# One change to a decoder-layer kernel on Trainium2: the down projection as a block product in seven products, with stored operand sums

## Chip, cores and metric

The kernel runs on one core of one Trainium2 chip. The metric is the device time of one execution in microseconds, the median of several runs.

## What is computed

One decoder layer for one sequence of 1024 tokens, width 1024, in fp32. Ahead of the part that matters here stand two attention groups, an output projection and a first layer norm. The change lies in the feed-forward block at the end, cut here to its core (D_FF = 2816):

```python
x  = layer_norm(ALPHA * x + (1 + gate_m) * y, ln1_g, ln1_b)
u2 = x * (1.0 + scale_f) + shift_f
h  = silu(u2 @ w_gate) * (u2 @ w_up)          # 1024 x 2816
y2 = h @ w_down                               # 1024 x 1024, inner dimension 2816
x  = layer_norm(ALPHA * x + (1 + gate_f) * y2, ln2_g, ln2_b)
```

## The kernel before

**Precision.** An fp32 matrix product is made from operands that are split in two: `split` (lines 86 to 88) has ScalarE cast a tile to the matmul type (`hi`, line 87) and VectorE subtract that from the tile (`lo`, line 88, two inputs in SBUF). Each product of two 128-row tiles then takes three matmuls (hi·hi, hi·lo, lo·hi), each 128x128 by 128x512.

**Gate/up.** The 2816 features are done in 22 groups of 128. Gate and up projection together are already a block product in seven products (`group_parts`, lines 1003 to 1051): 84 matmuls a group at line 996. For the next group `sum_weights` (lines 977 to 989) makes sums of weight blocks on VectorE (lines 982 to 985) and splits them. The results are put together in the tile `hf` by VectorE (lines 1032, 1040, 1042, 1043, 1047, 1048), and line 1049 stores `hf`, the hidden activations of 128 features by 1024 tokens, to DRAM (`h_d`).

**Down projection.** `ffn_down(half)` is called twice, for 512 tokens each. The eight PSUM accumulators are four row blocks q of 128 tokens by two column halves d of 512. A loop over 11 pairs of feature groups loads a pair of h back from `h_d` (line 1088) and both column halves of the matching 256 rows of w_down, splits these three tiles of 128x1024, and issues 48 matmuls (lines 1096 to 1098):

```python
h = (slot(HHI[n], (2, 512), dt=F32R, name="hh"), slot(HLO[n], (2, 512), dt=F32R, name="hl"))
load_h(i, *h)
w = [load_split((2, 512), w_src(i, d)) for d in range(2)]
for q in range(4):
    for d in range(2):
        mms(i, q, d, h, w[d])
```

That makes 2 x 11 x 48 = 1056 matmuls, and w_down is loaded twice. The last three pairs of a pass are kept in SBUF and multiplied one row block after the other, so that each row block ends by itself; then VectorE takes it out of PSUM times `gf` = 1 + gate_f (line 1138), adds it to ALPHA times the residual row (line 1139), takes statistics (line 824), and `out_norm` makes the layer norm and stores it (VectorE lines 829, 830, 1148, 1155; GpSimd's power for the inverse root, line 831, and its add at line 1153; ScalarE line 1152).

**The residual rows.** `rows_in(half)` (lines 1063 to 1072) loads four row blocks of z_d, the first layer norm without its gain and bias, and GpSimd multiplies by `l1g` (line 1069) and adds `l1b` (line 1070). Over both halves these are 16 GpSimd instructions of 128x1024.

**What sets the order.** The code is written in loops, but a scheduler arranges the instructions of each engine ahead of time; each engine then works in its fixed order and waits at semaphores. All loads and stores are issued in order from one queue (SP). Where a tile's place in SBUF (a numbered slot, or a pool's buffer) is used again, the load into it waits for the last reader.

Of the kernel before, what the change touches and what calls it, by code (L numbers as in the profile page):

```python
# [33 lines left out]
def hymba_layer_kernel(  # L34
# [967 lines left out]

    def group_parts(f, w):

# [17 lines left out]

        def p754():
            if f == 2:
                st_["h"] = slot(6 + par, (2, 512), name="hf")
# [31 lines left out]
    ROWS = ((0, 1, 2, 3), (10, 11, 12, 13))
    HRAW, HHI, HLO = (34, 35), (8, 16, 18), (9, 17, 19)
    NKEEP = 3
    KEPT = ((26, 27, 28, 29, 30, 31), (20, 21, 22, 23, 36, 37), (32, 33, 24, 25, 4, 5))  # L1060
# [13 lines left out]
    def ffn_down(half, between=()):
        last = half == 1
        between = list(between)
        wides = [wide(f"w{i}", "dn") for i in range(2)]
        acc = []
        for q in range(4):
            for d in range(2):  # L1080
                if q < 2:
                    acc.append(wides[q][:, d * 512 : (d + 1) * 512])
                else:
                    acc.append(bank(f"b{2 * (q - 2) + d}", "dn"))

        def load_h(i, hi, lo):
            raw = slot(HRAW[pc[0] % 2], (2, 512), name="hr")
            nc.sync.dma_start(raw, h_d[i][:, :, half * 512 : (half + 1) * 512].rearrange("f p n -> p f n"))
            split(hi, lo, raw)

        def mms(i, q, d, h, w):
            qs = slice(q * P, (q + 1) * P)
            for a in range(2):
                hh, hl, wh, wl = h[0][:, a, qs], h[1][:, a, qs], w[0][:, a, :], w[1][:, a, :]
                ps = acc[2 * q + d]
                nc.tensor.matmul(ps, hh, wh, start=i == 0 and a == 0, stop=False)  # L1096
                nc.tensor.matmul(ps, hh, wl, start=False, stop=False)  # L1097
                nc.tensor.matmul(ps, hl, wh, start=False, stop=i == NF // 2 - 1 and a == 1)  # L1098

        def w_src(i, d):  # L1100
            return w_down[i * 256 : (i + 1) * 256, d * 512 : (d + 1) * 512].rearrange("(k p) n -> p k n", p=P)

        for i in range(NF // 2 - NKEEP):
            n = pc[0] % 3
            h = (slot(HHI[n], (2, 512), dt=F32R, name="hh"), slot(HLO[n], (2, 512), dt=F32R, name="hl"))
            load_h(i, *h)
            pc[0] += 1
            w = [load_split((2, 512), w_src(i, d)) for d in range(2)]
            for q in range(4):
                for d in range(2):  # L1110
                    mms(i, q, d, h, w[d])
            if between:
                between.pop(0)()
        kept = []
        for n in range(NKEEP):
            i = NF // 2 - NKEEP + n
            ks = KEPT[n]
            h = (slot(ks[0], (2, 512), dt=F32R, name="kh"), slot(ks[1], (2, 512), dt=F32R, name="kl"))
            load_h(i, *h)
            pc[0] += 1  # L1120
            w = []
            for d in range(2):
                raw = wtile("raw", (2, 512), F32)
                nc.sync.dma_start(raw, w_src(i, d))
                hi = slot(ks[2 + 2 * d], (2, 512), dt=F32R, name="kwh")
                lo = slot(ks[3 + 2 * d], (2, 512), dt=F32R, name="kwl")
                split(hi, lo, raw)
                w.append((hi, lo))
            kept.append((i, h, w))
        rt = rows[half]  # L1130
        for q in range(4):
            bs = new_bs()
            for d in range(2):
                hs = slice(d * 512, (d + 1) * 512)
                for i, h, w in kept:
                    mms(i, q, d, h, w[d])
                tmp = tmp512("tmp")
                nc.vector.tensor_tensor(tmp, acc[2 * q + d], gf[:, hs], op=ALU.mult)
                nc.vector.scalar_tensor_tensor(
                    rt[q][:, hs], rt[q][:, hs], ALPHA, tmp, op0=ALU.mult, op1=ALU.add  # L1140
                )
                ln_stats(rt[q], d, bs)
            out_norm(half, q, rt[q], bs)
# [127 lines left out]
```

## Time and profile before

| | |
|---|---|
| Median of 3 runs | 1306.38 us (1302.6 to 1308.12) |
| Profiled execution | 1304.18 us, of which span 1302.4 us |
| Busy in the span | TensorE 96%, VectorE 58%, ScalarE 38%, GpSimd 20% |
| Mean granted TensorE clock | 0.996 of full speed |
| Gate/up, first matmul | 606.6 us |
| Down projection, first and last matmul | 1043.8 us, 1293.3 us |

Times in the trace count from the start of the span. PE is TensorE's matmul, DVE is VectorE, ACT is ScalarE, POOL is GpSimd, SP the queue that issues the loads and stores. A matmul's own duration (0.39 us) is longer than the distance between two starts, since they are pipelined; what a matmul costs is that distance.

### The profile page before, as it was taken

How to read it: one execution, taken by the hardware profiler on the slowest of the kernel's cores; microseconds unless marked ns; L12 is line 12 of the kernel's file. 1: busy time of each engine (PE TensorE's matmuls, PEld its weight loads, DVE VectorE, ACT ScalarE, POOL GpSimd, SP SyncE). 2: the span in 40 equal slices, each digit the busy share in tenths (PEclk: the TensorE clock that was granted, in tenths of full speed). 3: DMA queues.
4: the chain of work that ended last, by engine and by line, in shares of the span. 5: the costliest groups of instructions: out<-in, count | busy, mean ns of one | idle time of the engine just before them, and what ended most of it. 6: DMA issues, size and time to landing. Idle time of an engine off the chain costs nothing.

```text
span 1302.4 us, 16377 instructions
## 1 busy us (share of the span) xinstructions
PE 1256.3 (96%) x6341; PEld 1017.0 (78%) x6341; DVE 756.9 (58%) x1101; ACT 489.2 (38%) x826; POOL 259.6 (20%) x252
## 2 busy tenths in 40 slices
PE   5999999999999999998899999999999999999997
PEld 4888987899877656667688888888888888788885
DVE  7656537732465465456966565565566587483346
ACT  3422355523354465565633233233233333411331
POOL 3500023320255255331000000000000087010004
PEclk9999999999999999999999999999999999999999
DMA  9865621112125214144242331331231475643431
GB/s 299 260 226 180 213 65 34 27 23 66 50 91 145 74 34 147 65 145 130 82 144 81 98 96 51 96 97 54 93 97 49 167 267 164 201 153 116 148 111 65
DMA packets 124686, 153.17 MB, mean 118 GB/s; under 512 B 6608, under 2 KB 86586, under 8 KB 124608
## 3 DMA queue, kind: packets, MB, share of 16 engines
q1 hardware_dynamic: 124608, 152.12, 36.7%
q8 instruction: 50, 0.82, 0.3%
q14 instruction: 28, 0.23, 0.1%
HBM read 123.64 MB, written 24.13 MB: 113 GB/s over the span
## 4 chain that ended last, share of the span: by engine, by line
PE 75%; DMA 9%; DVE 7%; ACT 3%; issue 2%; POOL 2%; SPq 0%; POOLq 0%; DVEq 0%; ACTq 0%
PE gu L996 9%; PE gx L996 9%; PE gy L996 9%; DMA wc<-in_w_c_dram 5%; PE dn L1096 5%; PE dn L1098 5%; PE dn L1097 5%; PE gz L996 4%; PE pv L791 4%; PE tr L781 3%; PE acc L330 2%; PE acc L332 2%; PE acc L331 2%; PE acc L100 2%; DMA raw<-in_w_down_dram 2%
## 5 line engine op out<-in xcount | busy, mean ns | idle before, releaser
L88 DVE TENSOR_TENSOR lo<-raw,hi 128x1024 fp32r<-128x1024 f32 (+1 forms) x106 | 144.3, 1363 | 243.7 <-ACT hi L87 243.6
L87 ACT CAST hi<-raw 128x1024 fp32r<-128x1024 f32 (+1 forms) x106 | 110.8, 1048 | 204.8 <-PE dn L1098 83.2
L1069 POOL TENSOR_TENSOR r<-r,l1g 128x1024 f32<-128x1024 f32 x8 | 25.1, 3177 | 434.7 <-DVE hf L1040 434.7
L330 PE MATMUL acc<-hi,uh 128*128 128x264 f32 (+1 forms) x384 | 108.3, 283 | 1.4 <-ACT m L531 0.8
L331 PE MATMUL acc<-lo,uh 128*128 128x264 f32 (+1 forms) x384 | 108.2, 282 | 0.0
L332 PE MATMUL acc<-hi,ul 128*128 128x264 f32 (+1 forms) x384 | 108.2, 282 | 0.0
L1097 PE MATMUL dn<-lo,hh 128*128 128x512 f32 x256 | 100.9, 394 | 0.0
L1098 PE MATMUL dn<-hi,hl 128*128 128x512 f32 x256 | 100.5, 392 | 0.0
L1096 PE MATMUL dn<-hi,hh 128*128 128x512 f32 x256 | 94.3, 397 | 2.7 <-ACT hi L87 2.7
L330 PEld LDWEIGHTS acc<-hi,uh 128*128 128x128 f32 x384 | 72.2, 188 | 2.6 <-ACT m L531 1.0
L331 PEld LDWEIGHTS acc<-lo,uh 128*128 128x128 f32 x384 | 72.2, 188 | 0.6 <-issue 0.2
L332 PEld LDWEIGHTS acc<-hi,ul 128*128 128x128 f32 x384 | 72.2, 188 | 0.4 <-issue 0.2
L756 DVE CUSTOM_DVE_ANT_0 pr<-sc,smask 128x128 f32<-128x128 f32 (+7 forms) x64 | 47.7, 754 | 37.6 <-PE sc L752 22.8
L996 PE MATMUL gy<-s,b 128*128 128x512 f32 x264 | 64.8, 393 | 0.2 <-ACT s L87 0.2
L996 PE MATMUL gu<-a1h,lo 128*128 128x512 f32 x160 | 63.6, 397 | 0.0
L996 PE MATMUL gu<-a1l,hi 128*128 128x512 f32 x160 | 63.4, 396 | 0.0
L786 ACT COPY pt<-tr 128x512 f32<-128x512 f32 x80 | 45.6, 583 | 45.5 <-PE tr L781 38.6
L996 PE MATMUL gu<-a1h,hi 128*128 128x512 f32 x160 | 62.5, 390 | 0.0
L760 ACT ACTIVATE pr<-pr,sm 128x128 f32<-128x128 f32 (+7 forms) x64 | 49.8, 778 | 33.4 <-DVE sm L756 31.6
L996 PE MATMUL gz<-s,hi 128*128 128x512 f32 x176 | 59.5, 399 | 2.6 <-DVE s L88 2.6
L766 POOL TENSOR_SCALAR pr<-pr,sm 128x128 f32<-128x128 f32 (+7 forms) x64 | 51.5, 808 | 51.1 <-DVE sm L763 50.5
L791 PE MATMUL pv<-pt,fv 128*64 128x256 f32 x320 | 60.8, 395 | 0.7 <-DVE ofl L88 0.5
(306 smaller groups left out, 3030.8 us busy)
## 6 DMA issues: line engine op xcount, KB each, us to landing
raw<-in_w_down_dram SPq DMA_DIRECT2D x44, 512.0 KB, 4.9
wc<-in_w_c_dram SPq DMA_DIRECT2D x32, 512.0 KB, 4.3
raw<-in_w_gate_dram SPq DMA_DIRECT2D x25, 512.0 KB, 3.9
h_d<-hf SPq DMA_DIRECT2D x22, 512.0 KB, 2.8
hr<-h_d SPq DMA_DIRECT2D x22, 512.0 KB, 3.8
u<-in_w_up_dram SPq DMA_DIRECT2D x21, 512.0 KB, 3.9
wc<-in_w_c_dram SPq DMA_DIRECT2D x32, 256.0 KB, 6.5
raw<-in_w_in_dram SPq DMA_DIRECT2D x15, 512.0 KB, 4.0
```

Of the source, the lines that this page charges most:

```text
L87: nc.scalar.copy(dst_hi, src)
L88: return nc.vector.tensor_tensor(dst_lo, src, dst_hi.bitcast(F32), op=ALU.subtract).ins
L330: nc.tensor.matmul(ps, uh[k][:, ts], wh[:, k % 4, :], start=k == 0, stop=False)
L331: nc.tensor.matmul(ps, uh[k][:, ts], wl[:, k % 4, :], start=False, stop=False)
L332: nc.tensor.matmul(ps, ul[k][:, ts], wh[:, k % 4, :], start=False, stop=k == NK - 1)
L760: nc.scalar.activation(t[:, 0:nk], t[:, 0:nk], AF.Exp, bias=sm[:, 0:1], scale=-1.0, accum_out=sm[:, 1:2])
L766: nc.gpsimd.tensor_scalar(t[:, 0:nk], t[:, 0:nk], sm[:, 2:3], 1.0, op0=ALU.mult, op1=ALU.mult)
L791: nc.tensor.matmul(pv[64 * par : 64 * par + 64, 0:256], fv_t(kb)[:, 64 * h : 64 * h + 64], pt[:, par, a * 256 : (a + 1) * 256], start=kb == 0,
L996: nc.tensor.matmul(ps, x, y, start=start and j == 0 and i == 0, stop=j == NJ - 1 and i == 2, skip_group_check=not start,)
L1096: nc.tensor.matmul(ps, hh, wh, start=i == 0 and a == 0, stop=False)
L1097: nc.tensor.matmul(ps, hh, wl, start=False, stop=False)
L1098: nc.tensor.matmul(ps, hl, wh, start=False, stop=i == NF // 2 - 1 and a == 1)
```

## The change

The down projection becomes a block product in seven products. h is taken as 2x2 blocks (two halves of the tokens, even and odd feature groups), w_down likewise (even and odd feature groups, two column halves), and the seven products are each 512 x 1408 x 512: 11 inner tiles by 4 row blocks by 3 matmuls = 132 matmuls, 924 in all. The operand sums are made in fp32 and stored in DRAM while gate/up runs:

- `h_sums(i)`, after each pair of feature groups: four VectorE operations of 128x512 (lines 1022 to 1025) and four stores (lines 1027 and 1028) to `a_d[m][0..3]`, in place of the two stores to `h_d`.
- `w_sums(i)`, eleven times: two loads of w_down (line 1034), four VectorE operations of 128x512 (lines 1035 to 1038), two stores to `t_d` (line 1040). There is one pair of buffers for it (tags `c4b`, `c4c`).
- `ffn_down()` runs once, for all tokens. Each product has six groups; a group loads an a tile (line 1143) and a b tile (line 1145), splits both, and issues 24 matmuls (the sixth 12). Between the products, ScalarE copies partial results out of PSUM (`c1`, `c2`, `c5`; lines 1188, 1197, 1201), VectorE adds to them (lines 1192, 1206, 1210), and `add_rows` multiplies by `gf` on GpSimd (line 1180), adds to the residual row on VectorE (line 1181) and takes statistics. The four row blocks of half 0 are finished by the sixth product's end, those of half 1 one after the other from the seventh product (lines 1223, 1224).
- `l1g` and `l1b` are multiplied by ALPHA on ScalarE (lines 1320, 1321), ahead of GpSimd's rows (now lines 1109, 1110). Slots and constants lie elsewhere.

```diff
-                st_["h"] = slot(6 + par, (2, 512), name="hf")
+                st_["h"] = h_tile(f)
...
-            nc.sync.dma_start(h_d[f // 2][f % 2, :, :], h.rearrange("p a n -> p (a n)"))
+            if par == 1:
+                h_sums(f // 2)
...
+    def h_sums(i):
+        e, o = hs_.pop(2 * i), hs_.pop(2 * i + 1)
+        s23 = slot(34, (2, 512), name="hs")
+        s4 = slot(35, (512,), name="hs")
+        nc.vector.tensor_tensor(s23[:, 1, :], e[:, 0, :], e[:, 1, :], op=ALU.subtract)
+        nc.vector.tensor_tensor(e[:, 1, :], o[:, 1, :], e[:, 1, :], op=ALU.add)
+        nc.vector.tensor_tensor(s23[:, 0, :], e[:, 1, :], e[:, 0, :], op=ALU.subtract)
+        nc.vector.tensor_tensor(s4, o[:, 0, :], s23[:, 0, :], op=ALU.subtract)
+        for k, t in enumerate((e, o, s23)):
+            nc.sync.dma_start(a_d[i // 2][k][i % 2, :, :], t.rearrange("p a n -> p (a n)"))
+        nc.sync.dma_start(a_d[i // 2][3][i % 2, :, 0:512], s4)
+    def w_sums(i):
+        w0, w1 = [cp.tile([P, 2, 512], F32, tag=t, name=nm("wd")) for t in ("c4b", "c4c")]
+        for k, w in enumerate((w0, w1)):
+            nc.sync.dma_start(w.rearrange("p a n -> p (a n)"), w_down[(2 * i + k) * P : (2 * i + k + 1) * P, :])
...
+        for k, w in enumerate((w0, w1)):
+            nc.sync.dma_start(t_d[i // 2][i % 2, k, :, :], w.rearrange("p a n -> p (a n)"))
...
+        def product(banks, asrc, bsrc, new):
+            for m in range(NG):
+                g = group(m, asrc, bsrc)
+                for q in range(4):
+                    mms(banks[q], q, g, new and m == 0, m == NG - 1, new)
+        def add_rows(rt, bs, q, d, t):
+            hs = slice(d * 512, (d + 1) * 512)
+            nc.gpsimd.tensor_tensor(t, t, gf[:, hs], op=ALU.mult)
+            nc.vector.tensor_tensor(rt[q][:, hs], rt[q][:, hs], t, op=ALU.add)
+            ln_stats(rt[q], d, bs[q])
+        ra = rows_in(0)
+        product(sa, a_cols(0, 0), w_rows(0, 0), True)
...
+        product(sb, a_cols(3, 0), w_rows(1, 1), False)
+        for q in range(4):
+            nc.vector.tensor_tensor(c2[q], sb[q], c2[q], op=ALU.add)
+            add_rows(ra, bsa, q, 1, c2[q])
+            out_norm(0, q, ra[q], bsa[q])
+        asrc, bsrc = a_cols(1, 1), t_rows(1, 0)
+        for m in range(2):
+            g = group(m, asrc, bsrc)
+            for q in range(4):
+                mms(sa[q], q, g, False, False, False)
+        kept = [group(m, asrc, bsrc, True) for m in range(2, NG)]
         for q in range(4):
...
+            for g in kept:
+                mms(sa[q], q, g, False, g is kept[-1], False)
+            t = slot(30, (512,), name="tmp") if q % 2 else tmpb
+            nc.vector.tensor_tensor(t, sa[q], gf[:, 0:512], op=ALU.mult)
+            nc.vector.tensor_tensor(rb[q][:, 0:512], rb[q][:, 0:512], t, op=ALU.add)
+            ln_stats(rb[q], 0, bsb[q])
+            out_norm(1, q, rb[q], bsb[q])
...
+        if f >= 2 and f % 2 == 0:
+            w_sums(f // 2 - 1)
+    w_sums(NI - 1)
+    l1g = bcast(14, ln1_g, "l1g")
+    l1b = bcast(15, ln1_b, "l1b")
+    nc.scalar.mul(l1g, l1g, ALPHA)
+    nc.scalar.mul(l1b, l1b, ALPHA)
...
+    ffn_down()
```

The change also moves instructions, since the scheduler arranges each engine's list anew. Three places matter below. The first is VectorE where gate/up passes into the down projection. `hf` belongs to the last feature group; `hl`, `hr` (before) and `al`, `ar` (now) are the h operand's low half and its raw tile, `lo` the low half of a w_down tile. Before, from the group's first add to its last product:

```order
L1032 TENSOR_TENSOR hf_8337<-gy_8365,hf_8337 128x512 [waits DMAHW0_49,PE_49]
L88 TENSOR_TENSOR lo_8472<-raw_8469,hi_8471 128x1024 [waits DMAHW7_49,PE_49,Activation_49]
L1040 TENSOR_TENSOR hf_8337<-gz_8391,hf_8337 128x512 [waits PE_49]
L88 TENSOR_TENSOR lo_8532<-raw_8529,hi_8531 128x1024 [waits DMAHW2_49,Activation_49]
L1042 TENSOR_TENSOR sg_8405<-gx_8351,hf_8337 128x512 [waits DVE_49]
L1043 TENSOR_TENSOR hf_8337<-hf_8337 128x512
L88 TENSOR_TENSOR hl_8590<-hr_8591,hh_8589 128x1024 [waits DMAHW3_49,Activation_49]
L1047 TENSOR_TENSOR hf_8337<-gy_8365,hf_8337 128x512 [waits DVE_49,PE_49]
L1048 TENSOR_TENSOR hf_8337<-sg_8405,hf_8337 128x1024 [waits DVE_49,Activation_49]
```

Now, between the same two operations and on to the end of the pair's sums:

```order
L1071 TENSOR_TENSOR hf_8535<-gy_8563,hf_8535 128x512 [waits DMAHW3_49,PE_49]
L88 TENSOR_TENSOR al_8754<-ar_8749,ah_8753 128x1024 [waits DMAHW3_49,Activation_49]
L88 TENSOR_TENSOR lo_8720<-raw_8715,hi_8719 128x1024 [waits DMAHW1_49,PE_49,Activation_49]
L1079 TENSOR_TENSOR hf_8535<-gz_8589,hf_8535 128x512 [waits PE_49]
L88 TENSOR_TENSOR al_8718<-ar_8713,ah_8717 128x1024 [waits DMAHW4_49,Activation_49]
L88 TENSOR_TENSOR lo_8756<-raw_8751,hi_8755 128x1024 [waits DMAHW6_49,Activation_49]
L1081 TENSOR_TENSOR sg_8603<-gx_8549,hf_8535 128x512 [waits DVE_49]
L1082 TENSOR_TENSOR hf_8535<-hf_8535 128x512
L88 TENSOR_TENSOR al_8682<-ar_8677,ah_8681 128x1024 [waits DMAHW5_49,Activation_49]
L1086 TENSOR_TENSOR hf_8535<-gy_8563,hf_8535 128x512 [waits DVE_49,PE_49]
L1087 TENSOR_TENSOR hf_8535<-sg_8603,hf_8535 128x1024 [waits DVE_49,Activation_49]
L1025 TENSOR_TENSOR hs_8623<-hf_8535,hs_8622 128x512 [waits DVE_49]
```

Before, two w tiles and one h tile are split here, two further h tiles ahead of them. Now the a tiles of the first three groups of the first product are split here, that of the first group (`al_8682`) last, behind the other two, two w tiles and the operations of the feature group.

The second place is TensorE at the same point, from the last gate/up matmuls (line 996) to the first of the down projection (line 1167):

```order
L996 MATMUL gy_8563<-s_964_5750,b_1302_8520 128x512 x3
L996 MATMUL gy_8563<-s_965_5754,b_1302_8520 128x512 x3
L1167 MATMUL dn_8655<-hi_8683,ah_8681 128x512 [waits Activation_49]
L1167 MATMUL dn_8655<-lo_8684,ah_8681 128x512
L1167 MATMUL dn_8656<-hi_8683,ah_8681 128x512
L1167 MATMUL dn_8656<-lo_8684,ah_8681 128x512
L1167 MATMUL dn_8655<-hi_8683,al_8682 128x512 [waits DVE_49]
L1167 MATMUL dn_8655<-hi_8683,ah_8681 128x512
```

All gate/up matmuls stand ahead of the first of the down projection now, and the fifth of the down projection is the first that reads `al_8682`.

The third is VectorE in an early feature group, where the scheduler has put the sums of w_down (`wd`, lines 1035 to 1038) among the group's own work:

```order
L1035 TENSOR_TENSOR wd_6900<-wd_6900 128x512 [waits DMAHW6_49,DMAHW1_49]
L983 TENSOR_TENSOR u_6266<-u_6266 128x512 [waits DVE_49]
L1036 TENSOR_TENSOR wd_6900<-wd_6901,wd_6900 128x512 [waits DMAHW2_49,DVE_49]
L984 TENSOR_TENSOR u_6266<-u_6266,raw_6247 128x512 [waits DVE_49]
L1037 TENSOR_TENSOR wd_6901<-wd_6901,wd_6900 128x512 [waits DMAHW0_49,DVE_49]
L1071 TENSOR_TENSOR hf_6150<-gy_6178,hf_6150 128x512 [waits PE_49,Activation_49]
L985 TENSOR_TENSOR raw_6247<-raw_6247,u_6266 128x512 [waits DVE_49]
L1038 TENSOR_TENSOR wd_6901<-wd_6901 128x512 [waits DVE_49]
L88 TENSOR_TENSOR lo_6276<-u_6266,hi_6275 128x1024 [waits Activation_49]
L1082 TENSOR_TENSOR hf_6150<-hf_6150 128x512 [waits DVE_49]
L1035 TENSOR_TENSOR wd_7165<-wd_7165 128x512 [waits DMAHW4_49,DMAHW3_49]
```

The last row is the first operation of the next `w_sums`: it stands eight rows behind the one that last writes the same buffer (line 1036, `wd_6900`). All eleven `w_sums` stand in the lists of the first ten feature groups.

## Rows read from the trace of the kernel before

**Rows 1.** The profile's first part: busy time and share of each engine.
```profile
PE 1256.3 (96%) x6341; PEld 1017.0 (78%) x6341; DVE 756.9 (58%) x1101; ACT 489.2 (38%) x826; POOL 259.6 (20%) x252
```

**Rows 2.** The profile's fourth part: the chain that ended last, by engine.
```profile
PE 75%; DMA 9%; DVE 7%; ACT 3%; issue 2%; POOL 2%; SPq 0%; POOLq 0%; DVEq 0%; ACTq 0%
```

**Rows 3.** Waits of PE, 610 to 1302 us: us in total, times, longest.
```profile
PE dn L1096 <- ACT hi L87: 2.7, 1, 2.7
PE gz L996 <- DVE s L88: 2.6, 3, 0.9
```

**Rows 4.** Windows: busy us of each engine (instructions), granted clock, DMA share, GB/s.
```profile
core 0: us, PE busy (x) PEld busy (x) DVE busy (x) ACT busy (x) POOL busy (x), PEclk, DMA share, GB/s
...
700.00:800.00 100.00, 100.00 (x434) 81.39 (x433) 57.85 (x73) 30.34 (x42) 0.00 (x0) 1.00 0.29 94
...
1060.00:1100.00 40.00, 40.00 (x175) 32.61 (x175) 33.49 (x11) 9.96 (x10) 37.59 (x12) 1.00 0.50 160
1100.00:1150.00 50.00, 47.19 (x199) 37.88 (x198) 26.70 (x24) 20.52 (x21) 0.00 (x0) 0.97 0.67 214
1150.00:1200.00 50.00, 50.00 (x220) 41.05 (x219) 32.66 (x48) 6.10 (x6) 6.08 (x4) 1.00 0.31 106
```

**Rows 5.** The tile `dn`: ns min/median/max, first and last start.
```profile
L1096 PE MATMUL dn<-hi,hh x256: 387/392/786, 1043.8 to 1260.2; 128*128 128x512 f32 x128
L1098 PE MATMUL dn<-kwh,kl x96: 388/389/398, 1139.8 to 1293.3; 128*128 128x512 f32 x96
```

**Rows 6.** Timeline of DVE in a gate/up group: start us, us, operation, idle before it.
```profile
747.58 1.23 DVE L88 TENSOR_TENSOR lo<-raw,hi 128x1024 fp32r<-128x1024 f32 x1 [6.99 <-ACT hi L87]
...
750.34 0.69 DVE L983 TENSOR_TENSOR u<-u 128x512 f32<-128x512 f32 x1
```

**Rows 7.** DMA issues: count, KB each, median us to landing.
```profile
raw<-in_w_down_dram SPq DMA_DIRECT2D x44, 512.0 KB, 4.9
h_d<-hf SPq DMA_DIRECT2D x22, 512.0 KB, 2.8
...
r<-z_d SPq DMA_DIRECT2D x8, 512.0 KB, 8.4
```

**Rows 8.** Timeline of DVE at the start of the down projection.
```profile
1045.44 1.22 DVE L88 TENSOR_TENSOR lo<-raw,hi 128x1024 fp32r<-128x1024 f32 x1
...
1047.17 2.30 DVE L1043 TENSOR_TENSOR hf<-hf 128x512 f32<-128x512 f32 x1
...
1052.75 0.68 DVE L1047 TENSOR_TENSOR hf<-gy,hf 128x512 f32<-128x512 f32 x1
1053.53 2.64 DVE L1048 TENSOR_TENSOR hf<-sg,hf 128x1024 f32<-128x1024 f32 x1
...
1059.45 3.42 DVE L88 TENSOR_TENSOR hl<-hr,hh 128x1024 fp32r<-128x1024 f32 x1
1062.79 3.42 DVE L88 TENSOR_TENSOR lo<-raw,hi 128x1024 fp32r<-128x1024 f32 x1
```

**Rows 9.** Timeline of POOL in the same stretch, and line 1069 by duration.
```profile
1045.70 25.15 POOL L1069 TENSOR_TENSOR r<-r,l1g 128x1024 f32<-128x1024 f32 x8 [434.73 <-DVE hf L1040]
1070.81 26.78 POOL L1070 TENSOR_TENSOR r<-r,l1b 128x1024 f32<-128x1024 f32 x8
...
L1069 POOL TENSOR_TENSOR r<-r,l1g x8: 2407/3382/3397, 1045.7 to 1068.4; 128x1024 f32<-128x1024 f32 x8
```

**Rows 10.** Timeline of DVE and POOL behind the last matmul, and line 1153 by duration.
```profile
1293.74 0.69 DVE L1138 TENSOR_TENSOR tmp<-dn,gf 128x512 f32<-128x512 f32 x1 [1.93 <-PE dn L1098]
...
1295.19 0.69 DVE L824 BATCH_NORM_STATS2 bs<-r 128x6 f32<-128x512 f32 x1
...
1296.23 1.28 DVE L1148 SCALAR_TENSOR_TENSOR r<-r,mv,l2g 128x1024 f32<-128x1024 f32 x1
1297.95 1.41 DVE L1155 SCALAR_TENSOR_TENSOR r<-r,mv,l2b 128x512 f32<-128x512 f32 x2 [0.44 <-POOL mv L831]
...
1296.46 1.46 POOL L831 TENSOR_TENSOR mv<-mv,half_neg 128x1 f32<-128x1 f32 x1 [2.98 <-DVE mv L830]
...
L1153 POOL TENSOR_TENSOR r<-r,l2b x6: 1295/1570/2400, 1279.5 to 1292.2; 128x512 f32<-128x512 f32 x6
```

More of the change, by code (lines that the diff above doesn't have):

```diff
@@ L1024, in p754 @@
             if f == 2:
[L1025 removed]
+                st_["h"] = h_tile(f)
             h = st_["h"]
@@ L1054, in hymba_layer_kernel @@
     HG = (14, 15)
[L1057 to L1060, printed above, removed]
+    ROWS = ((28, 20, 1, 12), (29, 21, 10, 27))
+    HRAW, HHI, HLO = (32, 33, 18), (8, 16, 0), (9, 17, 11)
+    KEPT = {2: (31, 23, 3, 25), 3: (4, 5, 6, 7), 4: (34, 35, "c4a", 19), 5: (None,) * 4}
     pc = [0]
@@ L1072, in rows_in @@
         return rt
[L1074 to L1078, printed above, removed]
-        for q in range(4):
[L1080 to L1108, printed above, removed]
-            for q in range(4):
[L1110 to L1130, printed above, removed]
-        for q in range(4):
[L1132 to L1143, printed above, removed]
@@ new lines, in any_tile, with ffn_down, group, mms @@
+    def any_tile(i, shape, dt, name):
+        if isinstance(i, str):
+            return cp.tile([P, *shape], dt, tag=i, name=nm(name))
+        return slot(i, shape, dt=dt, name=name)
+    def ffn_down():
+        wides = [wide(f"w{1 - i}", "dn") for i in range(2)]
+        sa = [wides[q // 2][:, (q % 2) * 512 : (q % 2 + 1) * 512] for q in range(4)]
+        sb = [bank(f"b{q}", "dn") for q in range(4)]
+        def group(m, asrc, bsrc, keep=False):
+            n = 2 if m < NG - 1 else NI - 2 * (NG - 1)
+            raw = slot(HRAW[pc[0] % 3], (n, 512), name="ar")
+            nc.sync.dma_start(raw, asrc(m, n))
+            braw = wtile("raw", (n, 512), F32)
+            nc.sync.dma_start(braw, bsrc(m, n))
+            if keep and n == 1:
+                at = cp.tile([P, 2, 512], F32R, tag="c4b", name=nm("ka"))
+                bt = cp.tile([P, 2, 512], F32R, tag="c4c", name=nm("kb"))
+                ah, al, bh, bl = at[:, 0:1, :], at[:, 1:2, :], bt[:, 0:1, :], bt[:, 1:2, :]
+            elif keep:
+                ah, al, bh, bl = [any_tile(i, (n, 512), F32R, "kp") for i in KEPT[m]]
+            else:
+                ah = slot(HHI[pc[0] % 3], (n, 512), dt=F32R, name="ah")
+                al = slot(HLO[pc[0] % 3], (n, 512), dt=F32R, name="al")
+                bh, bl = wtile("hi", (n, 512), F32R), wtile("lo", (n, 512), F32R)
+            split(ah, al, raw)
+            split(bh, bl, braw)
+            pc[0] += 1
+            return n, ah, al, bh, bl
+        def mms(ps, q, g, start, stop, new):
+            n, ah, al, bh, bl = g
+            qs = slice(q * P, (q + 1) * P)
+            for a in range(n):
+                tr = ((ah, bh), (ah, bl), (al, bh))
+                for i, (x, y) in enumerate(tr):
+                    nc.tensor.matmul(
+                        ps, x[:, a, qs], y[:, a, :], start=start and a == 0 and i == 0,
+                        stop=stop and a == n - 1 and i == 2, skip_group_check=not new,
+                    )
+        def product(banks, asrc, bsrc, new):
[10 more added lines that the diff above has]
+        product(sa, a_cols(0, 0), w_rows(0, 0), True)
+        c1 = halves((36, 37))
+        for q in range(4):
+            nc.scalar.copy(c1[q], sa[q])
+        product(sb, a_cols(1, 0), w_rows(1, 0), True)
+        bsa = [new_bs() for q in range(4)]
+        for q in range(4):
+            nc.vector.tensor_tensor(c1[q], sb[q], c1[q], op=ALU.add)
+            add_rows(ra, bsa, q, 0, c1[q])
+        product(sa, a_cols(2, 0), t_rows(1, 1), False)
+        c2 = halves((2, 13))
+        for q in range(4):
+            nc.scalar.copy(c2[q], sa[q])
+        product(sb, a_cols(0, 1), t_rows(0, 0), True)
+        c5 = halves((36, 37))
+        for q in range(4):
+            nc.scalar.copy(c5[q], sb[q])
+        rb = rows_in(1)
+        product(sa, a_cols(2, 1), t_rows(0, 1), False)
+        bsb = [new_bs() for q in range(4)]
+        for q in range(4):
+            nc.vector.tensor_tensor(c5[q], sa[q], c5[q], op=ALU.add)
+            add_rows(rb, bsb, q, 1, c5[q])
+        product(sb, a_cols(3, 0), w_rows(1, 1), False)
+        for q in range(4):
+            nc.vector.tensor_tensor(c2[q], sb[q], c2[q], op=ALU.add)
[4 more added lines that the diff above has]
+            g = group(m, asrc, bsrc)
+            for q in range(4):
+                mms(sa[q], q, g, False, False, False)
+        kept = [group(m, asrc, bsrc, True) for m in range(2, NG)]
+        for q in range(4):
+            for g in kept:
[5 more added lines that the diff above has]
+            out_norm(1, q, rb[q], bsb[q])
```

45 lines of the change are left out of this document (33 added, 12 removed).

## The prediction

> **What bounds the kernel now.** I read the busy shares first: PE is busy 96% of the span, every other engine far less [rows 1]. The chain that ended last says the same: 75% of it is PE [rows 2]. Then the waits of PE in the part that changes: from 610 us on the two largest are 2.7 us, once in the down projection, and 2.6 us in three pieces [rows 3]. The windows show where other engines come near: in a stretch of gate/up DVE works 57.85 of 100 us, but between 1060 and 1100 us, with POOL on the residual rows, DVE is busy 33.49 of 40 us for only eleven instructions [rows 4]. So fewer matmuls shorten the time as long as DVE can feed PE, and the question is where it no longer can.
>
> **PE.** In full windows a matmul takes 50.00/220 = 0.227 us (down projection), 40.00/175 = 0.229 (the boundary) or 100.00/434 = 0.230 (gate/up) [rows 4]. The change does 924 matmuls for 1056, 132 fewer. At 0.2286 us that is **−30.2 us** (−30.0 to −30.4). The wait of 2.7 us in the down projection belongs to the old arrangement and goes too [rows 3]; in its window the granted clock was 0.97, so 3% of 50 us is missing and costs 1.5 us [rows 4]: **−4.2 us**.
> By the Trainium skill, "TensorE: Matmul & The Clock Gate", section "Back-to-back issue gap", a warm matmul of 512 columns follows the one before it after 215.7 ns. The saving by that would be an estimated 28.5 us. The trace shows 0.227 to 0.230, so I keep the row.
>
> **Gate/up.** An operation of 128x512 takes 0.69 us, a split of 128x1024 1.23 [rows 6]. A group of 84 matmuls lasts 84 x 0.230 = 19.4 us, in which DVE now works 57.85% = 11.2 us. h sums add four operations per pair, 1.4 us per group; w sums add 4 x 0.69 = 2.8 us to each of the first ten groups. DVE then stands at 15.4 of 19.4 us. Its idle time is mostly one gap per group, such as 6.99 us ahead of 747.58 [rows 6], which takes the 4.2 us. The stores and loads come to an issue for the load wait: a `w_sums` may begin only after the store (2.8 us) and the next load (4.9 us) have gone through the one buffer [rows 7], 7.7 us against eight operations in between (5.5 us). The 2 us left fall partly into the gap. I take **+1.5 us** (0 to +8).
>
> **The boundary.** Let E be the end of the last gate/up matmul. Before, matmuls of the down projection stood ahead of it: the first started at 1043.8 us [rows 5], while the last addition of gate/up came at 1052.75 [rows 8]. Now none does, and the fifth matmul behind E reads `al_8682`. The a tiles go into slots that gate/up operands hold until about 38 matmuls ahead of E (8.7 us), and their loads stand in the queue behind l1g and three residual rows. With 4.9 us to land the first comes at E − 4. From there DVE has five splits of 1024 to do up to `al_8682`, and with them two operations that read PSUM and one of 512 with both inputs in SBUF.
> What these cost depends on POOL. Before POOL starts (1045.70 [rows 9]) a split takes 1.22 us; while it multiplies residual rows one takes 3.42, the next starting 3.34 us later (1059.45, 1062.79), and line 1043 takes 2.30; line 1047, with an input in PSUM, still takes 0.68 [rows 8]. POOL suffers likewise: its shortest instruction took 2.41 us, the median 3.38 [rows 9]. The two engines alternate. In the new order POOL's eight multiplications come when rows and l1g have landed, about E − 5, on the same five splits. Contended: 5 x 3.35 + 2.3 + 2 x 0.7 = 20.4 us, `al_8682` at E + 16.4. Not contended: 5 x 1.2 + 3 x 0.65 = 8 us, E + 4. PE has 0.9 us of work of its own there. The stall is 3 to 15.5 us; I take 14, near the contended end, since POOL's block of 8 x 3.4 = 27 us covers the whole stretch and the rows of the same kind of work all show it. The clock adds 1.5, as with the old stall [rows 4]: **+15.5 us** (+3 to +19).
> The Trainium skill, "SBUF — State Buffer", section "Who interferes with whom", explains the alternation: a DVE instruction with two SBUF inputs and a GpSimd instruction that reads SBUF exclude each other for a whole instruction, and one of the two "fully blocks". By that a split would wait for a whole POOL multiplication, 2.41 + 1.22 = 3.63 us; the rows show 3.35. Five times the difference is 1.4 us more stall.
>
> **POOL's second block.** The eight additions of l1b wait for ScalarE's ALPHA * l1b, whose place in its list is behind casts that wait for PE in the first product. They run beside the splits of the first products: two of these per 24 matmuls (5.5 us) then take 6.7 us. The excess over some 27 us is up to 6; splits done ahead cover half: **+3 us** (0 to +6).
>
> **The middle.** Four splits per 48 matmuls (11 us) are 4.9 us, where before there were three; with additions and statistics DVE has 11 splits (13.5 us) and up to twelve operations of 0.69 us, 22 of 30 us per product. Loads: seven products move about 40 MB in 211 us, 190 GB/s; the old window of 1100 to 1150 moved 214 GB/s with the queues' share at 0.67 [rows 4]. Covered both: 0.
>
> **The tail.** Let T be the start of the seventh product. PE needs 132 x 0.2286 = 30.2 us for it. From T on DVE has: six splits of 1024 and one of 512 (8.1 us), four additions to c2 and four to the rows (5.5), four statistics (2.8), the layer norm of four rows of half 0 (4 x 1.28 and 4 x 1.41 = 10.8, and 1.2 of small ones), then four rows of half 1, each with 0.69 (out of PSUM), 0.69 (add), 0.69 (statistics), 1.28 and small ones (3.7), 14.8 in all, and 1.41 for the last [rows 6, 10]. That is 44.6 us, with waits on POOL's multiplications (1.30 to 2.40 each, line 1153's size) and on the inverse roots (1.46) about 48, beginning 2 us ahead of T, where the first banks of the sixth product are done. DVE ends near T + 46.5, 16 us behind the last matmul. Before it was 1299.36 − 1293.7 = 5.7 us [rows 5, 10]. **+10.5 us** (+6 to +14): here DVE takes PE's place as the bound.
>
> **Sum.** −30.2 − 4.2 + 1.5 + 15.5 + 3 + 10.5 = −3.9 us. The profiled execution took 1304.2 us, 2.2 below the median of the runs: 1300.3 against it, **1302.5 us** against 1306.38.
>
> **The rivals.** 0.5%, 6.5 us, is about what a measurement of this kernel can tell from no change.
> A, DVE's new work is hidden: the residual rows land late, so that POOL starts after `al_8682`, and the tail's adds are done in time. −30.2 − 4.2 + 0 + 3 + 1.5 + 0 + 6 = −23.9: 1282.5 us. For it: in gate/up DVE has 40% free. Against: the order of DVE's list, and that rows of z_d took 8.4 us to land in a crowd [rows 7], which delays the a tiles behind them as well.
> B, slower, by one mechanism: the single buffer of `w_sums`. DVE works in order; if store and load take longer than the operations between and the gap, the splits of the next group's weights come late and PE stops in each of ten groups. It decides from a round trip of 5.5 + 4 = 9.5 us on. The load time of 8.4 us that the z_d rows had, with 2.8 for the store, makes 11.2, 1.7 us more, and as much again in clock and lost alignment: 10 x 2.5 = 25 us in place of 1.5. Sum +19.6: 1326 us. Against: the queues were busy only 0.29 of the time there [rows 4].
> C, between B and the forecast: boundary and tail at their upper ends 3 more each for gate/up and POOL, −3.9 + 3.5 + 3.5 + 3 + 3 = +9.1: 1315.5 us.
> D, the change does not do what it says. The order shows seven products of 132 matmuls, so I give it nothing.
>
> **Chances.** Forecast (within 8 us) 0.45, A and what lies toward it 0.28, B 0.10, C 0.17. Faster by over 0.5% (under 1299.9): A, and 0.10 of the forecast's own spread, 0.38. Within 0.5%: 0.36. Slower (over 1312.9): B and C less what falls inside, 0.26. The range leaves out A's far end and B: 1283 to 1320; the forecast's own is 1294 to 1311.
>
> **What would show it.** The boundary: PE idle some 14 us behind the last gate/up matmul, waiting for DVE's `al`, splits of 3.4 us around it. The tail: DVE without gaps over the last 45 us, ending some 16 us behind the last matmul. Gate/up: PE still full between 700 and 1000 us. I am wrong if PE waits in gate/up at lines 996, if the boundary's splits take 1.2 us, or if the seventh product waits for loads.

## The result and the profile after

The changed kernel took 1315.94 us (median of 6 runs, 1312.9 to 1318.48) against 1306.41 us before: a ratio of 1.0077, with a 95% interval of 1.0055 to 1.0098. It is slower by 9.5 us, where I had forecast 3.9 us less. The time lies inside the range, and on the side to which I had given 0.26. One of all the executions, one of the ten in e1_spread below, took 2040.64 us at a granted clock of 0.56; no ratio counts it, and without it the median given there is 1304.77 us.

The first part of the profile and its chain, the lines that answer to [rows 1, 2]:

```profile
PE 1240.2 (94%) x6209; PEld 996.8 (76%) x6209; DVE 826.6 (63%) x1207; ACT 507.6 (39%) x858; POOL 275.9 (21%) x264
...
PE 66%; DMA 13%; DVE 10%; issue 3%; ACT 3%; POOL 3%; SPq 1%; POOLq 0%; DVEq 0%; ACTq 0%
```

PE is busy for 16 us less and the span is 12 us longer, 1314.4 us. In the chain PE's share has fallen from 75% to 66%; DMA and DVE have taken it. The waits of PE from 600 us on, the view of [rows 3], name where:

```profile
PE dn L1167 <- DVE al L88: 13.6, 3, 11.8
PE dn L1167 <- DVE lo L88: 3.5, 2, 2.6
PE gz L996 <- DVE lo L88: 3.0, 3, 1.6
PE gu L996 <- DVE lo L88: 2.3, 3, 1.2
PE dn L1167 <- DVE tmpb L1223: 1.7, 1, 1.7
```

In nearly all of them what PE waited for was an operation of DVE, at three places: in gate/up (line 996), at the boundary (11.8 us), and in the seventh product. The windows, as in [rows 4], show the first two. In gate/up DVE's busy time went up from 57.85 to 80.72 us and PE lost 5.7; at the boundary the granted clock (PEclk, the last figure but two) fell as well, from 1.00 to 0.83:

```profile
core 0: us, PE busy (x) PEld busy (x) DVE busy (x) ACT busy (x) POOL busy (x), PEclk, DMA share, GB/s
...
700.00:800.00 100.00, 94.34 (x400) 74.12 (x399) 80.72 (x111) 30.27 (x41) 0.00 (x0) 1.00 0.79 265
...
1060.00:1100.00 40.00, 28.23 (x111) 22.70 (x111) 25.32 (x16) 8.21 (x9) 21.73 (x9) 0.83 0.76 255
```

**Gate/up.** A marker fixes its loss: the product that ends feature group 20 on DVE. It started at 1029.50 us before,

```profile
1029.50 1.23 DVE L1048 TENSOR_TENSOR hf<-sg,hf 128x1024 f32<-128x1024 f32 x1
```

and at 1041.06 us in the changed kernel:

```profile
1041.06 1.23 DVE L1087 TENSOR_TENSOR hf<-sg,hf 128x1024 f32<-128x1024 f32 x1
```

That is 11.6 us later, of which 2.4 were there when gate/up began (its first matmul at 609.0 for 606.6, behind code that is the same). So gate/up lost **9.2 us**. DVE's own list of waits, 640 to 860 us, and its timeline show what held it:

```profile
DVE wd L1035 <- DMA wd<-in_w_down_dram: 19.7, 10, 4.4
...
DVE wd L1036 <- DMA wd<-in_w_down_dram: 6.6, 7, 1.6
```

```profile
759.19 0.69 DVE L1035 TENSOR_TENSOR wd<-wd 128x512 f32<-128x512 f32 x1 [4.35 <-DMA wd<-in_w_down_dram]
759.80 1.22 DVE L88 TENSOR_TENSOR lo<-raw,hi 128x1024 fp32r<-128x1024 f32 x1
```

At 759.19 DVE had waited 4.35 us for a load of w_down while the split that PE needed stood next in its list; PE waited in turn:

```profile
761.08 0.50 PE L996 MATMUL gu<-a1h,lo 128*128 128x512 f32 x1 [1.16 <-DVE lo L88]
```

DVE stood 26.3 us in front of its own first two operations of `w_sums`, waiting for w_down. The queue's own waits, from 600 to 1100 us, show what these loads (line 1034) waited for in turn, the landing of the store out of the same buffers:

```profile
SPq L1034 <- DMA t_d<-wd: 45.2, 16, 5.5
```

That the held-up queue made gate/up's own weights late does not show: ScalarE, which casts them, waited for no load between 640 and 860 us.

The DMA issues give the round trip (medians), to be read against [rows 7]: the store of a sum took 5.2 us, where the store of h had taken 2.8, and the next load 4.4.

```profile
wd<-in_w_down_dram SPq DMA_DIRECT2D x22, 512.0 KB, 4.4
t_d<-wd SPq DMA_DIRECT2D x22, 512.0 KB, 5.2
```

**The boundary.** DVE and POOL, as in [rows 8, 9], and the matmul that waits:

```profile
1055.21 2.81 DVE L88 TENSOR_TENSOR al<-ar,ah 128x1024 fp32r<-128x1024 f32 x1 [2.30 <-ACT ah L87]
1057.94 1.21 DVE L88 TENSOR_TENSOR lo<-raw,hi 128x1024 fp32r<-128x1024 f32 x1
...
1059.68 2.94 DVE L88 TENSOR_TENSOR al<-ar,ah 128x1024 fp32r<-128x1024 f32 x1
1062.54 3.35 DVE L88 TENSOR_TENSOR lo<-raw,hi 128x1024 fp32r<-128x1024 f32 x1
...
1068.57 3.36 DVE L88 TENSOR_TENSOR al<-ar,ah 128x1024 fp32r<-128x1024 f32 x1
...
1048.83 8.11 POOL L1109 TENSOR_TENSOR r<-r,l1g 128x1024 f32<-128x1024 f32 x3 [435.51 <-PE gu L996]
1059.17 14.99 POOL L1109 TENSOR_TENSOR r<-r,l1g 128x1024 f32<-128x1024 f32 x5 [2.24 <-DVE lo L88]
...
1071.98 0.80 PE L1167 MATMUL dn<-hi,al 128*128 128x512 f32 x1 [11.77 <-DVE al L88]
1072.58 0.63 PE L1167 MATMUL dn<-hi,ah 128*128 128x512 f32 x1
1073.00 0.63 PE L1167 MATMUL dn<-lo,ah 128*128 128x512 f32 x1
```

This is the picture that was forecast: four of the five splits take 2.8 to 3.4 us beside POOL, the one that falls into POOL's pause (1056.94 to 1059.17) takes 1.21. Behind the wait the matmuls come 0.43 us apart for 6 us, in place of 0.23; the granted clock there (1072 to 1077 us) was 0.50, which is 1.2 GHz.

POOL's additions of l1b ran beside the second product, and three short waits of PE fall into them, 2.7 us in all. The longest:

```profile
1092.43 23.25 POOL L1110 TENSOR_TENSOR r<-r,l1b 128x1024 f32<-128x1024 f32 x8 [18.27 <-ACT l1b L1321]
...
1113.48 0.50 PE L1167 MATMUL dn<-hi,al 128*128 128x512 f32 x1 [1.35 <-DVE al L88]
```

**The end.** In the seventh product PE waits 2.58 us for a split, then runs some 13 matmuls at 0.43 us, and waits 1.74 us once more for `tmpb`. The row of 1298.60 holds the last matmuls, the row of 1309.90 the last DVE operations, as in [rows 5, 10]:

```profile
1269.97 0.80 PE L1167 MATMUL dn<-lo,ah 128*128 128x512 f32 x1 [2.58 <-DVE lo L88]
1270.57 0.63 PE L1167 MATMUL dn<-hi,al 128*128 128x512 f32 x1
...
1289.49 4.40 PE L1167 MATMUL dn<-kp,kp 128*128 128x512 f32 x18 [1.74 <-DVE tmpb L1223]
...
1298.60 0.87 PE L1167 MATMUL dn<-kb,ka 128*128 128x512 f32 x3
...
1309.90 1.41 DVE L1238 SCALAR_TENSOR_TENSOR r<-r,mv,l2b 128x512 f32<-128x512 f32 x2 [1.66 <-POOL mv L831]
```

DVE ends at 1311.3, 11.8 us behind the last matmul (1299.5), where it was 5.7.

The two waits in the seventh product differ in what lies behind them. Around the start of this product (first matmul at 1260.7 us) DVE was not working through a full list: it stood idle for 7.46 and then for 2.38 us in front of splits whose casts on ScalarE were waiting for loads of a tiles (`kp` are the operands of the last groups, kept in SBUF). The split that PE waited for (1268.22) is the fifth operation from the end of the second idle time on, with no idle time between:

```profile
1256.38 1.23 DVE L88 TENSOR_TENSOR kp<-ar,kp 128x1024 fp32r<-128x1024 f32 x1 [7.46 <-ACT kp L87]
...
1264.75 1.23 DVE L88 TENSOR_TENSOR kp<-ar,kp 128x1024 fp32r<-128x1024 f32 x1 [2.38 <-ACT kp L87]
...
1268.22 1.70 DVE L88 TENSOR_TENSOR lo<-raw,hi 128x1024 fp32r<-128x1024 f32 x1
...
1263.66 1.05 ACT L87 CAST kp<-ar 128x1024 fp32r<-128x1024 f32 x1 [2.62 <-DMA ar<-a_d]
```

So a late load stands at the head of the wait of 2.58 us. The later one, for `tmpb`, is a wait for DVE's list: from 1264.75 us to its end DVE's longest gap is the 1.66 us shown above.

**The account**, span against span (1314.4 − 1302.4 = +12.0 us). A matmul's excess is its distance to the next one less 0.2295 us, summed over the rows at a place:

| | forecast | measured |
|---|---|---|
| ahead of gate/up | 0 | +2.4 |
| gate/up | +1.5 | +9.2 |
| 132 matmuls fewer | −30.2 | −30.3 |
| the old wait and its clock | −4.2 | −4.2 |
| boundary, with the clock | +15.5 | +15.6 |
| POOL's second block | +3 | +3.5 |
| seventh product, waits and clock | (in the end) | +8.1 |
| DVE behind the last matmul | +10.5 | +6.2 |
| rest (matmuls 0.230 us apart for 0.229) | 0 | +1.5 |

### The profile page after: what moved, and what is told of

It is laid out like the page before. It is cut to its first block, busy times and chain, and to the rows that moved or that the text cites. A ratio compares the mean times of both kernels' runs of the same rounds, so it can differ in the third digit from the quotient of the medians.

```text
span 1314.4 us, 16515 instructions
## 1 busy us (share of the span) xinstructions
PE 1240.2 (94%) x6209; PEld 996.8 (76%) x6209; DVE 826.6 (63%) x1207; ACT 507.6 (39%) x858; POOL 275.9 (21%) x264
## 3 DMA queue, kind: packets, MB, share of 16 engines
q1 hardware_dynamic: 137216, 189.61, 45.2%
## 4 chain that ended last, share of the span: by engine, by line
PE 66%; DMA 13%; DVE 10%; issue 3%; ACT 3%; POOL 3%; SPq 1%; POOLq 0%; DVEq 0%; ACTq 0%
PE dn L1167 12%; PE gu L996 7%; PE gy L996 6%; PE gx L996 6%; PE pv L791 4%; DMA t_d<-wd 3%; DMA wc<-in_w_c_dram 3%; PE gz L996 3%; DMA wd<-in_w_down_dram 3%; PE tr L781 3%; PE acc L330 3%; PE acc L332 3%; PE acc L331 3%; PE acc L100 2%; PE acc L99 2%
## 5 line engine op out<-in xcount | busy, mean ns | idle before, releaser
L87 ACT CAST hi<-raw 128x1024 fp32r<-128x1024 f32 (+1 forms) x112 | 114.8, 1026 | 134.4 <-PE gu L996 46.1
L1167 PE MATMUL dn<-hi,al 128*128 128x512 f32 x280 | 111.1, 402 | 13.6 <-DVE al L88 13.6
L1167 PE MATMUL dn<-lo,ah 128*128 128x512 f32 x280 | 112.4, 401 | 3.5 <-DVE lo L88 3.5
L1167 PE MATMUL dn<-hi,ah 128*128 128x512 f32 x280 | 110.9, 401 | 1.1 <-ACT ah L87 0.8
L88 DVE TENSOR_TENSOR al<-ar,ah 128x1024 fp32r<-128x1024 f32 (+1 forms) x38 | 58.2, 1539 | 50.6 <-ACT ah L87 50.5
L1167 PEld LDWEIGHTS dn<-hi,al 128*128 128x128 f32 x280 | 54.0, 193 | 27.7 <-DVE al L88 14.9
L87 ACT CAST ah<-ar 128x1024 fp32r<-128x1024 f32 (+1 forms) x38 | 37.3, 984 | 88.2 <-PE dn L1167 83.4
L1167 PEld LDWEIGHTS dn<-lo,ah 128*128 128x128 f32 x280 | 54.0, 193 | 16.6 <-DVE lo L88 4.3
L1167 PEld LDWEIGHTS dn<-hi,ah 128*128 128x128 f32 x280 | 53.8, 192 | 14.3 <-ACT ah L87 1.2
```

The lines of the kernel that those rows point to most:

```text
L87: nc.scalar.copy(dst_hi, src)
L88: return nc.vector.tensor_tensor(dst_lo, src, dst_hi.bitcast(F32), op=ALU.subtract).ins
L1167: nc.tensor.matmul(ps, x[:, a, qs], y[:, a, :], start=start and a == 0 and i == 0, stop=stop and a == n - 1 and i == 2, skip_group_check=n ...
```

## The experiments

The theory on which the experiments were built: three separate losses eat the 30 us, all of them waits of PE for DVE's list. In gate/up DVE stands in front of loads that go round through one buffer; at the boundary it shares with POOL; at the end it has more work than PE. Each has a rival. The first four runs change one thing each in the changed kernel (1315.9 us).

### e1_spread: the sums of w_down, one to every second feature group

```diff
-        if f >= 2 and f % 2 == 0:
-            w_sums(f // 2 - 1)
-    w_sums(NI - 1)
+        if f == 0 or (f % 2 == 1 and f < NF - 2):
+            with after(f"h{f}"):
+                w_sums((f + 1) // 2)
```

(`after` places what follows behind the product that ends group f.)

> The eleven w_sums are put one into every second feature group, behind that group's hidden activations, in place of the first ten groups; all else as in the changed kernel (1315.9 us). My theory: in the changed kernel VectorE waits in order for the loads of w_down into the one pair of buffers (26 us of such waits between 640 and 860 us) and PE loses 9 us of gate/up to it. Spread, a store and a load have two groups (39 us) to land: PE's waits at line 996 behind 640 us fall from about 8 us to under 2, gate/up ends 7 to 9 us earlier, 1307 to 1309 us. Rival, the transfers themselves (75 MB more in the whole kernel) slow gate/up's own loads: the same bytes are moved, so at most a third is gained, 1313 us or more.

Measured: 1305.01 us, ratio to before 0.9992 (0.9977 to 1.0007), 2 us below what I expected. DVE waited for w_down once, 3.4 us:

```profile
DVE wd L1036 <- DMA wd<-in_w_down_dram: 3.4, 1, 3.4
```

Group 20 ended at 1030.73 us, 10.3 us earlier, 9.2 if each is counted from its own first gate/up matmul (607.9 and 609.0), which is all that gate/up had lost. Another 2 us were gained in the first two products, which I had not counted on. The same bytes (189.6 MB for 152.1 before in the whole kernel, half the increase that I had written down) and the same operations cost nothing once they are spread. So neither they nor the bandwidth were the loss; where they stood was. The loads still waited for the stores (the queue's waits for `t_d` at line 1034 from 600 to 1100 us are 37.9 us here, 45.2 before the sums were spread), but DVE no longer stood waiting behind them.

### e1_nostore: the round trip alone

```diff
-        for k, w in enumerate((w0, w1)):
-            nc.sync.dma_start(t_d[i // 2][i % 2, k, :, :], w.rearrange("p a n -> p (a n)"))
...
-        return lambda m, n: t_d[m][0:n, k, :, c * 512 : (c + 1) * 512].rearrange("i p n -> p i n")
+        return w_rows(k, c)
```

> As the changed kernel, but w_sums does not store its sums, and the products that used them load plain rows of w_down in their place. Loads, VectorE operations and their number in gate/up stay. My theory (the round trip of store and load through one buffer): the next load needs only wait for VectorE, 4.4 us in place of 9.6, so VectorE's waits for wd fall to under a third of 26 us and gate/up gains 5 to 9 us: 1307 to 1311 us. Rival, VectorE has too much work in the first ten groups: its operations are all there, so nothing is gained, 1314 to 1318 us.

This run leaves the sums of w_down out of the products, so its output is not the layer's; it serves for the time alone. Measured: 1307.41 us, ratio 1.0012 (1.0002 to 1.0023), 8.5 us less than the changed kernel; group 20, counted from the first gate/up matmul, ended 8.3 us earlier. DVE did the same operations in the same early groups, and its waits for w_down fell from 26.3 to 7.5 us:

```profile
DVE wd L1035 <- DMA wd<-in_w_down_dram: 4.7, 4, 2.9
DVE wd L1036 <- DMA wd<-in_w_down_dram: 2.8, 5, 1.3
```

The window that had lost 5.7 us is full again, with DVE as busy as in the changed kernel (80.70 us for 80.72):

```profile
700.00:800.00 100.00, 100.00 (x434) 81.43 (x433) 80.70 (x110) 31.19 (x43) 0.00 (x0) 1.00 0.53 173
```

So it was not the amount of DVE's work. What held the load back was the store ahead of it in the same buffer; the queue's waits for `t_d` are gone with it. This run does not part the store's own landing time from the share of the queues that the stores took; both go with it.

### e2_drows: no GpSimd at the boundary

```diff
-            nc.gpsimd.tensor_tensor(r, r, l1g, op=ALU.mult)
-            nc.gpsimd.tensor_tensor(r, r, l1b, op=ALU.add)
...
+            if 5 <= pc[0] < 13:
+                r = (ra + rb)[pc[0] - 5]
+                with tc.issue_after(ins):
+                    nc.vector.tensor_tensor(r, r, l1g, op=ALU.mult)
+                    nc.vector.tensor_tensor(r, r, l1b, op=ALU.add)
...
-        ra = rows_in(0)
+        ra, rb = rows_in(0), rows_in(1)
...
-        rb = rows_in(1)
```

> The sixteen operations on the residual rows go from GpSimd to VectorE, one row behind the splits of each of the groups five to twelve of the down projection; the loads and the order at the boundary stay. My theory (the two engines exclude each other): the splits at the boundary take 1.2 us in place of 2.8 to 3.4, the fifth down matmul waits 3 to 4 us in place of 11.8, and with the clock 9 to 11 us are gained there; 16 x 1.2 = 20 us more for VectorE in the first products costs 0 to 4. Sum 1305 to 1310 us. Rival, the a tiles are loaded too late: the splits get short, but the wait stays at 9 us or more, and the time at 1314 us or more.

Measured: 1299.01 us, ratio 0.9946 (0.9926 to 0.9966), 16.9 us less than the changed kernel, and 6 below the range that I expected, which had left out POOL's second block. The loads at the boundary stood in the same order (the rows of half 1 were loaded there in the changed kernel too), and the split and the matmul behind it read:

```profile
1061.33 1.22 DVE L88 TENSOR_TENSOR al<-ar,ah 128x1024 fp32r<-128x1024 f32 x1
...
1062.60 0.54 PE L1170 MATMUL dn<-hi,al 128*128 128x512 f32 x1 [2.61 <-DVE al L88]
```

All five splits took 1.22 or 1.23 us and the wait fell from 11.77 to 2.61 us. The waits of POOL's second block went too: from 1050 to 1130 us PE waited only these 2.6 us. The splits, with two inputs in SBUF, took 2.8 to 3.4 us beside POOL and 1.22 without it, while the operations that read PSUM (lines 1079, 1081 and 1086) took 0.68 us in both. This agrees with the Trainium skill, "SBUF — State Buffer", section "Who interferes with whom", by which a VectorE instruction with two SBUF inputs contends with a GpSimd instruction that reads SBUF, and one with at most one does not. DVE's 16 operations more (20 us) cost the PE nothing that shows: products two to six lost 1.2 us together, 4.2 in the changed kernel.

### e3_swap: half 0's rows out of the last product

The blocks of the fifth product (with its additions) and of the sixth change places:

```diff
+        product(sb, a_cols(3, 0), w_rows(1, 1), False)
...
         product(sa, a_cols(2, 1), t_rows(0, 1), False)
...
-        product(sb, a_cols(3, 0), w_rows(1, 1), False)
```

> The fifth and the sixth product change places, so that the four rows of half 0 are finished during the product before the last; no operation more or less. My theory (VectorE is the bound at the end, with 45 us of work for a product of 30): the 12 us of layer norm of half 0 leave the end, VectorE ends 6 us behind the last matmul in place of 11.8, and PE's stall of 4.6 us with its clock loss of 2.6 in the seventh product halves: 8 to 11 us gained, less 1 to 2 for the sixth product that follows on the same banks: 1306 to 1309 us. Rival, the seventh product waits for its loads: they are as late as before, so its stall stays, and at most 5 us are gained: 1311 us or more.

Measured: 1310.57 us, ratio 1.0042 (1.0027 to 1.0058), 5.4 us less, half of what I expected. The interval (1309.4 to 1313.5 us) does not part this from the rival's 1311, so the trace has to tell. In the changed kernel DVE had done the layer norm of half 0 during the seventh product, not ahead of it (line 1231, from 1281.08 us on); here that work left the seventh product, and DVE ended 8.9 us behind the last matmul for 11.8. But a new wait took the place of the old one:

```profile
PE dn L1167 <- DVE dc L1211: 5.3, 1, 5.3
```

The seventh product goes on in the PSUM banks of the fifth, which now comes directly ahead of it, and PE has to wait until DVE has read them (line 1211). In DVE's list those reads stood behind five splits for the seventh product. The wait of 2.58 us for a split, with a late load at its head, and the one for `tmpb` are gone. The rival's stall did not stay, then, but the run moves DVE's work and the times of the loads together, so it does not show how much of the old stall was due to which.

### e3_tie: the reads of PSUM ahead of those splits

```diff
         for m in range(2):
-            g = group(m, asrc, bsrc)
+            with after("c5") if m else nullcontext():
+                g = group(m, asrc, bsrc)
...
-        kept = [group(m, asrc, bsrc, True) for m in range(2, NG)]
+        with after("c5"):
+            kept = [group(m, asrc, bsrc, True) for m in range(2, NG)]
```

(on top of e3_swap; `c5` is the last of the four reads.)

> e3_swap, and in the seventh product the splits of all groups behind the first stand behind the four additions that read the fifth product out of PSUM. In e3_swap PE waited 5.3 us for these additions, since five splits stood ahead of them. If VectorE's order alone caused that wait, it falls to under 2 us and the clock stays up: 1303 to 1307 us against 1310.6. Rival: the wait is for the banks themselves, since the product goes on accumulating where the one before ended; then it stays above 4 us and the time at 1309 us or more.

Measured: 1307.25 us, ratio 1.0011 (0.9996 to 1.0026), 3.3 us less than e3_swap and at the upper end of what I expected. The wait fell to 1.9 us, as DVE's order alone would have it:

```profile
PE dn L1167 <- DVE dc L1211: 1.9, 1, 1.9
```

Swap and order together give 8.7 us.

### c1_two: spread sums and rows on VectorE

> e1_spread and e2_drows together. If the two losses are separate, in gate/up by the waits for w_down and at the boundary by the exclusion of VectorE and GpSimd, the gains add: 1315.9 - 10.9 - 16.9 = 1288 us (1286 to 1291), gate/up ends about 1046 us in the trace and the wait at the boundary stays at 3 us. If one covers part of the other, 1293 us or more.

Measured: 1293.66 us, ratio 0.99 (0.9873 to 0.9927): 22.3 us less, not 27.8, and nominally on the rival's side, though the interval (1290 to 1297 us) decides nothing. The trace has both gains at their places: group 20 ends at 1031.63 us (1030.73 in e1_spread), and the wait at the boundary is 2.6 us. By the spans of the two runs the sum would be 1287.9 us, and it is 1293.0. Of these 5.1 us, 1.4 lie ahead of gate/up, whose first matmul came between 606.5 and 609.0 us in executions of the same code, and 1.4 behind the last matmul (DVE ends 11.6 us behind it, 10.4 in e2_drows). Another 2.8 lie at the boundary and in the first two products, where e1_spread had already shortened by 2.3 us what e2_drows takes away too: there one gain covers part of the other. The seventh product is 0.4 us off the sum, and gate/up ended 1.0 us better.

### c3_all: all of it

> All of it: w_sums spread, the residual rows on VectorE, fifth and sixth product changed and the order of e3_tie. If the three losses add, c1_two less the 9 to 11 us of the end: 1276 to 1281 us, 2% below the kernel before, and what is left of the change is its 132 matmuls less. If VectorE, which now has all of the residual rows, is short at the end or in the middle, 1284 us or more, with waits of PE at line numbers of the down projection of over 8 us.

Measured: 1283.72 us, ratio **0.9825 (0.9798 to 0.9851)**: 22.9 us less than before and 32.2 less than the changed kernel. It lies above the 1276 to 1281 us that I expected: the step from c1_two is 9.9 us, as expected, but the sum starts from a c1_two that was itself short by 5.7. PE's largest waits from 600 us on, and the window that had lost 5.7 us:

```profile
PE gz L996 <- DVE s L88: 2.7, 3, 1.0
PE dn L1170 <- DVE al L88: 2.6, 1, 2.6
PE dn L1170 <- DVE dc L1213: 1.9, 1, 1.9
```

```profile
700.00:800.00 100.00, 100.00 (x434) 81.47 (x433) 72.64 (x97) 30.01 (x41) 0.00 (x0) 1.00 0.53 175
```

The rival named waits of over 8 us in the down projection; there are 5.0. What is still lost: DVE ends 9.4 us behind the last matmul (1268.95 and 1278.34), 3.7 more than before, the first product loses 4.5 us, and the wait ahead of the seventh with the product itself 4.7.

## Why the prediction was wrong

- **PE, −30.2 us.** Right: 132 matmuls at the rate of the rows. The matmuls left came 0.230 us apart, which cost about 1.5 us.
- **Gate/up, +1.5 us.** This is the first step that failed: the term measured +9.2. I had the mechanism (one buffer, store and load between two `w_sums`, DVE in order), set the round trip at 2.8 + 4.9 = 7.7 us, and wrote that the 2 us left "fall partly into the gap". The trip took 5.2 + 4.4 = 9.6 us, because the store took 2.4 us longer; I had taken its time from a kernel whose queues were busy 0.29 of the time in gate/up, and with the change it was 0.79. But the longer trip is not enough to explain the price: by my own rule (nothing lost up to 9.5 us) it would have cost 0.1 us a group. The overlap was wrong. DVE waited 26.3 us, and the gap hid only part of that: the wait stood in DVE's list ahead of the split that ends the gap, so that it delayed what the gap was there for, and PE lost 9.2 us, beyond the +8 that I had as its end. e1_spread and e1_nostore took the loss away in two ways.
- **Rival B** named this mechanism and set the point from which it decides at 9.5 us. It was passed, yet the price was 9 us and not 25: DVE waited 26 us, but what reached PE is a third of that. (The 25 does not follow from its own terms either: 1.7 us and as much again are 3.4 a group, 34 in all.) Rival C gave the time, 1315.5 us, by other terms (the boundary at its end, where it came as forecast, and 4.5 us for gate/up), so its number is luck and no confirmation.
- **The boundary, +15.5 us.** Right in place and cause. The size, 15.6, is right by parts that cancel: 11.8 us of wait and 0.75 ahead of it make 12.5 for the 14 I took, and the rest, 3 us of clock, is twice my 1.5, which came from one old stall. e2_drows showed the cause, and the uncontended wait of 3 us that I gave as the lower end was 2.6.
- **POOL's second block, +3 us.** Right: 3.5, and gone in e2_drows.
- **The tail, +10.5 us.** The second step that failed. It was right that DVE is the bound at the very end: from 1264.75 us on it worked for 46.6 us with one gap of 1.7. But I took the seventh product as full (30.2 us), and it lasted 38.6, since PE waited within it. I had put nothing for late loads there. DVE stood idle 9.8 us around its start for them, and a late load heads the wait of 2.58 us that, with its clock, makes 5.4 of the 8.1 us; the 1.74 us for `tmpb` is DVE's list. So the sign that I had named against myself, a seventh product that waits for loads, showed for the larger part of this loss, one step behind DVE. e3_swap and e3_tie removed both waits together; how the 5.4 us divide between the load and DVE's order stays open. With the 6.2 us behind the last matmul the loss is 14.3, just above the +14 I had as an end.
- **Against the median**: of the 12.0 us between the two profiled executions 2.4 lie ahead of the changed part, so the medians, 9.5 apart, fit the terms better than the spans do.

## What to carry to other kernels

A saving on the bound engine is worth what the engine that feeds it can keep up with at each place, and a share of the whole span does not tell: DVE was at 58%, and three stretches gave back all of the 30 us. Work that is put into the gaps of an engine that keeps its order should not wait for anything there, since a waiting instruction holds up the one behind it; put it where its inputs have long landed. With DVE 81% busy either way, gate/up lost 9.2 us while the loads waited for stores (changed kernel) and 0.9 when they did not (e1_nostore). And when an engine seems too busy to keep up, look for idle time in its own list first: here some of the wait for DVE was a wait for loads. And before work is moved beside GpSimd, look whether both engines read SBUF in the same stretch.

## What the runs showed of the hardware

- A store of 512 KB to DRAM took 2.8 us (median, kernel before) where 94 GB/s were moved in gate/up, 3.4 us at 176 GB/s (e1_spread) and 5.2 us at 265 GB/s (changed kernel; rates from 700 to 800 us).
- Behind a wait PE ran at a granted clock of 0.50 (1.2 GHz) for a while, and the loss did not grow with the wait: in the changed kernel the clock cost 2.9 us behind 2.6 us (seventh product) and 2.9 behind 11.8 (boundary). Other runs lost less behind the same waits at the boundary, 1.4 us behind 2.6 in c3_all and 2.1 behind 12.6 in e3_tie, and the wait of 2.9 us for `tmpb` in e1_nostore cost none (clock 1.00 from 1278 to 1284 us).
- A VectorE subtraction of 128x1024 with both inputs in SBUF took 1.22 us alone and 2.8 to 3.4 beside GpSimd's multiplications; one of 128x512 with an input in PSUM took 0.68 us in both cases.
- 20 us more of fp32 operations on VectorE in the first products, with two inputs in SBUF and no GpSimd beside them, cost nothing that shows; with the same operations on GpSimd the kernel took 16.9 us more.
